# Modulation weights of the latent feed-forwards loaded through GpSimd's queue, their sums ordered behind the newest low part

## The chip, the core and the metric

One core of a Trainium2 chip runs the whole program. The metric is the time of one execution on the device in microseconds (us). Three timed runs of the kernel before are shown, and one more execution was profiled.

## The reference

Two layers run over 256 latent tokens of width 1024 (with 256 context tokens in the first layer only). Each layer is feed-forward, mixer, feed-forward, and each of these three is wrapped the same way:

```python
def sublayer(h, m, i, fn, res_w):
    y = fn(modulate(h, m[3 * i], m[3 * i + 1]))        # h * (1 + scale) + shift
    return layer_norm(ALPHA * h + res_w * m[3 * i + 2] * y, ln_g[l, i], ln_b[l, i])

def swiglu(h, w_in, w_out):                            # 1024 -> 2 x 2816 -> 1024
    gate, up = jnp.split(h @ w_in, 2, axis=-1)
    return (jax.nn.silu(gate) * up) @ w_out

m_lat = jnp.split(silu(c) @ w_ada[l] + b_ada[l], 9)    # nine vectors of 1024 a layer
```

The nine modulation vectors of a layer are products of one row, silu(c), with a 1024 x 9216 matrix. All numbers are float32.

## The kernel before

Every large matrix product is done in three passes: weights and activations are each split into a high part (rounded to the fast format) and a low part (the rest), and TensorE adds high x high, high x low and low x high (`mm3`, L209). A weight load brings 128 x 2048 floats (1 MB) into one of three buffers `raw` (L129, on SyncE's queue). ScalarE casts 1024 columns of it into `wh` (L150), VectorE subtracts and so makes the low part `wl` (L151). Here 1024 columns with their `wh` and `wl` are called a weight part; six buffers each hold them, and `wnext` makes parts five ahead of the one in use (`AHEAD`).

A latent feed-forward (`sub_ffn` and `ffn` with T = 2; there are three, in the order (0,1), (1,0), (1,1)) uses 66 weight parts: 44 for the first product, four to a pair of columns `ff`, and 22 for the second. TensorE makes `lf` (gate and up for 128 tokens), ScalarE applies SiLU and VectorE multiplies (`lsgf`, L469 and L470), TensorE transposes the product a little later (`ltrf`, `turn_last`, L435), and it is split again.

Beside this run the modulation vectors of later steps. `ada_jobs` lists them: for each vector eight units, and a unit is a load of 128 x 1024 floats (512 KB, `load`, L236, tile `ada`) and a sum on VectorE (`unit`, L240): the load times the row silu(c), summed over the 1024. After eight units `fin` (L248 on) adds the bias on GpSimd, and for a gate sends the vector to memory and back to spread it over the partitions (`gd`, `grow`). In the latent feed-forwards there are two buffers for the loads (`NADS`). `pace(44)` spreads the listed sums evenly over 44 steps. `bgstep` counts a step after each weight part from the third pair of columns on, that is from the 9th part, and calls `bg_one` when a sum is due; this issues the loads of the next two units and the sum.

At the start of a latent feed-forward `flush` (L377) puts out the scaling of `h` by the gain and bias of the layer norm before, `affine` (L368): on GpSimd, for each of two token tiles, a load of the gain row (512 KB, L372), two products, a load of the bias row into the same buffer, and two additions (L375). They stand behind `last_pow`, which there is GpSimd's share of the split of the normalized tokens (L217).

The order on each engine's queue is fixed when the program is put together: an instruction that is ready early can stand in front of one that is written earlier. `tc.issue_after(i)` puts what is written inside it behind instruction i, if it is on the same engine. `behind_x` does so for the split of the tokens.

Of the kernel before, what the change touches and what calls it, by code (L numbers as in the profile page):

```python
# [66 lines left out]
def body(ctx: ExitStack, tc: tile.TileContext, out, a):  # L67
    nc = tc.nc
    act, dve, pool, pe = nc.scalar, nc.vector, nc.gpsimd, nc.tensor
# [12 lines left out]
    def mmt(name):  # L82
        return mmp.tile([P, 512], F32, tag="mm", name=name)
# [16 lines left out]
    def col(name, i=0, n=1):  # L100
        return cols[:, CO[name] + i: CO[name] + i + n]
# [12 lines left out]
    ready = []  # L114
# [22 lines left out]
    lo_ins = {}  # L137
# [84 lines left out]
    bg = []  # L222
    cur_ada = [None]
    NADS = [3]

    def ada_jobs(l, v, streams, gate=None, then=None):


        for s in streams:
            mcol[l, v, s] = colp.tile([P, 8], F32, name=f"m{l}{v}{s}")  # L230
        for j in range(8):
            st = {}

            def load(j=j, st=st):
                st["raw"] = cur_ada[0].tile([P, D], F32, tag="adaraw", name=f"ada{l}{v}{j}", bufs=NADS[0])
                nc.sync.dma_start(st["raw"], a["wada"][l, v, j])  # L236

            def unit(j=j, st=st):
                for s in streams:
                    dve.scalar_tensor_tensor(st["raw"] if s == streams[-1] else crow["junk"], st["raw"], 1.0, crow[s], ALU.mult, ALU.mult,  # L240
                                             accum_out=mcol[l, v, s][:, j:j + 1])

            bg.append((load, unit, len(streams)))

        def fin():
            for s in streams:
                m = mcol[l, v, s]
                pool.tensor_tensor(m, m, col("bad", (l * 9 + v) * 8, 8), ALU.add)  # L248
                if gate is None:
                    continue  # L250
                if gate != 1.0:
                    pool.tensor_scalar(m, m, gate, None, ALU.mult)

                dr = drp.tile([P, 8], F32, name=f"gd{l}{v}{s}")
                pool.dma_start(dr, m)
                mrow[l, v, s] = (rowp if v == 5 else cur_ada[0]).tile([P, D], F32, tag=f"grow{s}", name=f"grow{l}{v}{s}", bufs=1)
                pool.dma_start(mrow[l, v, s], dr.rearrange("p j -> (p j)").partition_broadcast(P))
            if then is not None:
                then()

        bg.append((None, fin, 0))

    rate = [0.0, 0.0]

    def bg_one():
        for pre, _, _ in bg[:NADS[0]]:
            if pre is not None and id(pre) not in done:
                done[id(pre)] = pre
                pre()
        with behind_x():  # L270
            bg.pop(0)[1]()


# [2 lines left out]
    @contextmanager  # L276
    def behind_x():
        with ExitStack() as st:
            for i in anchors:
                st.enter_context(tc.issue_after(i.ins))  # L280
            yield
# [84 lines left out]
    last_pow = [None]  # L366
# [10 lines left out]
    def flush(after=None):  # L377
        with tc.issue_after((after or last_pow[0]).ins):
            while later:
                later.pop(0)()  # L380
# [19 lines left out]
    def ffn(st, l, i, T, parts, gv, prep, finish, lead):  # L400
# [43 lines left out]
        for p0, p1 in parts:  # L444
            for ff in range(p0, p1, 2):
                q = ff - p0
                if T == 4:
                    for j in range(2):
                        if ff + j in pre:
                            gps, ups = pre.pop(ff + j)  # L450
                        else:
                            gps, ups = mmt(f"g{nm}{ff}{j}"), mmt(f"u{nm}{ff}{j}")
                            group(gps)
                            group(ups)
                        act_mul(gps, ups, gslice(q + j, 1, slice(0, W)), 1, f"{nm}{ff}{j}")
                elif ff % 4 == 0 or ff > LEAD:

                    pairs = [ff, ff + 2] if ff < LEAD else [ff]
                    ps = {(f, t): mmt(f"l{nm}{f}{t}") for f in pairs for t in range(T)}
                    sg = {f: tp.tile([P, T, 256], F32, tag="t2", bufs=2, name=f"lsg{nm}{f}") for f in pairs}  # L460
                    ws = {}
                    seq = [(ff, t, j) for j in range(4) for t in range(T)]
                    if len(pairs) > 1:

                        seq = [(f, t, j) for t in range(T) for f in pairs for j in range(4) if f == ff or j < 2]
                        seq += [(ff + 2, t, j) for j in (2, 3) for t in range(T)]

                    def gate(f, t):
                        act.activation(sg[f][:, t, :], ps[f, t][:, 0:256], AF.Silu)  # L469
                        dve.tensor_tensor(sg[f][:, t, :], sg[f][:, t, :], ps[f, t][:, 256:512], ALU.mult)  # L470

                    for f, t, j in seq:
                        if (f, j) not in ws:
                            ws[f, j] = wnext((4, 3, 2, 1, 2, 1)[len(ws)] if ff == 0 and len(ws) < 6 else AHEAD)
                            if ff:
                                bgstep()
                        for k in (2 * j, 2 * j + 1):
                            with ExitStack() as after:
                                if ff == 0 and k % 2 == 0 and (f, t, j) != seq[0]:
                                    after.enter_context(tc.issue_after(last_mm[0].ins))  # L480
                                out_mm(ps[f, t], t, XH, XL, 0, k, k % 2, ws[f, j], k == 0, k == KT - 1)
                        if (f, t, j) == (0, 0, 3) and pend:
                            with behind_x(), tc.issue_after(nrm[0].ins):
                                pump_split(taken[0] + 2)
                            with tc.high_priority(HP), tc.issue_after(last_mm[0].ins):
                                to_x(*pend.pop())

                        if (f, t, j) == (2, 0, 1):
                            with behind_x():
                                gate(0, 0)  # L490
                        if j == 3 and (f, t) != (0, 0):
                            gate(f, t)
                            if t == T - 1:
                                turn_last()
                                turns.append((sg[f], q + f - ff, f))
                    if ff == 0:
                        flush()
            final = p1 == NFF
            for n in range(2):
                if final and n == 1:  # L500
                    while bg:
                        bg_one()
                    prep()
                pss = [mmt(f"o{nm}{p0}{n}{t}") for t in range(T)]
                qs = list(range(p0, p1, 2))
                hold = []
                for qi, k0 in enumerate(qs):
                    hold.append((k0, wnext(AHEAD + max(0, qi - 8) if T == 2 and final and n == 1 else AHEAD)))
                    bgstep()
                    if qi == 2:  # L510
                        turn_last()
                    if final and n == 1 and len(qs) - HOLD <= qi < len(qs) - 1:
                        continue
                    for t in range(T):
                        for kq, w in hold:
                            for kk in range(2):
                                gh, gl = gslice(kq + kk - p0, 1, slice(t * P, (t + 1) * P))
                                out_mm(pss[t], 0, gh, gl, 0, 0, kk, w, kq == p0 and kk == 0, kq == qs[-1] and kk == 1)
                        if qi == len(qs) - 1:
                            with tc.high_priority(HP if final else 0):  # L520
                                evac(pss[t], t, n, mrow[gv(t)], final and n == 1, ALPHA if p0 == 0 else 1.0,
                                     f"{nm}{p0}{n}{t}", f"{nm}{t}" if final else None)
                                if final and n == 1:
                                    finish(t)
                    hold = []
# [108 lines left out]
    with ExitStack() as st1:  # L634
# [38 lines left out]
        def prep():  # L673
            pass
# [242 lines left out]
    def sub_ffn(l, i, gates, mods, ln, nxt):  # L917
        with ExitStack() as st:
            cur_ada[0] = st.enter_context(tc.tile_pool(name=f"ada{l}{i}", bufs=1, side="right"))
            NADS[0] = 2  # L920
            for (gl, gv, f) in gates:
                ada_jobs(gl, gv, (0,), gate=f)
            for ml, mi, mln in mods:
# [368 lines left out]
```

## Time and profile before

| | us |
|---|---|
| timed runs | 1233.27, 1236.50, 1236.87 |
| median | 1236.5 |
| profiled execution | 1233.74 |
| its span, first instruction to last | 1231.9 |
| first latent feed-forward, about | 526 to 708 |
| second latent feed-forward, about | 715 to 906 |
| third latent feed-forward, about | 1037 to 1224 |

The profile is of one execution. An engine is busy while it runs an instruction; the time between two instructions is put down to what released the second one. PE is TensorE (PEld its weight loads), DVE VectorE, ACT ScalarE, POOL GpSimd, SP SyncE, which issues DMAs. PEclk is the granted share of TensorE's full clock of 2.4 GHz; 0.50 is 1.2 GHz. Times of a row count from the start of the span.

### The profile page before, as it was taken

The numbers are of one execution on the slowest core, as the hardware profiler recorded it, in microseconds if no ns is written. First come the engines' busy times: TensorE is split into PE (matmuls) and PEld (weight loads), VectorE is DVE, ScalarE is ACT, GpSimd is POOL, SyncE is SP. The second block draws the span as 40 slices with busy tenths as digits, with TensorE's granted clock in tenths as the row PEclk, the third lists the DMA queues.
The fourth block names the chain that finished last, engine by engine and source line by source line (L and its number), as shares of the span: only waits on it lengthen the run. The fifth ranks groups of instructions, "written<-read, shape, count | busy, mean of one in ns | idle before, by whom it ended". The sixth has DMA issues, their size and how long they took to land.

```text
span 1231.9 us, 14930 instructions
## 1 busy us (share of the span) xinstructions
PE 1181.1 (96%) x5632; PEld 979.7 (80%) x5632; DVE 882.7 (72%) x1287; ACT 503.2 (41%) x731; POOL 206.7 (17%) x207
## 2 busy tenths in 40 slices
PE   6999999999999999999999999997999888999997
PEld 5888888888887887778888878886879877888885
DVE  5799987773337858798785688877667957875554
ACT  4243123222233546564444444433448333544431
POOL 0001020031003122134010033000017911330000
PEclk9899999999999999999999999998999989999999
DMA  9778688862232432369885748987648445975550
GB/s 361 306 252 290 230 275 308 271 223 100 86 124 65 161 137 103 137 233 336 329 299 186 265 167 337 326 315 274 220 164 297 145 178 168 322 279 184 175 188 35
DMA packets 59656, 272.60 MB, mean 221 GB/s; under 512 B 6592, under 2 KB 8256, under 8 KB 44224
## 3 DMA queue, kind: packets, MB, share of 16 engines
q1 hardware_dynamic: 56048, 259.56, 59.2%
q0 software_dynamic: 3536, 12.09, 3.0%
q8 instruction: 44, 0.72, 0.2%
q14 instruction: 28, 0.23, 0.1%
HBM read 269.38 MB, written 1.08 MB: 220 GB/s over the span
## 4 chain that ended last, share of the span: by engine, by line
PE 48%; DVE 7%; DMA 6%; ACT 2%; issue 2%; POOL 1%; DVEq 0%; SPq 0%; ACTq 0%; POOLq 0%
PE lf L212 7%; PE lf L210 6%; PE lf L211 6%; DMA ada<-in_wada 6%; PE of L210 4%; PE of L212 4%; PE of L211 4%; PE pc L1137 2%; DVE wl L151 2%; DVE ada L240 1%; PE c L210 1%; PE c L211 1%; PE c L212 1%; PE ltrf L435 1%; PE v L210 1%
## 5 line engine op out<-in xcount | busy, mean ns | idle before, releaser
L150 ACT CAST wh<-raw 128x1024 fp32r<-128x1024 f32 x309 | 321.6, 1051 | 466.6 <-PE of L212 128.3
L151 DVE TENSOR_TENSOR wl<-raw,wh 128x1024 fp32r<-128x1024 f32 x302 | 379.2, 1271 | 150.3 <-ACT wh L150 149.3
L210 PE MATMUL lf<-wh,XH 128*128 128x512 f32 x528 | 208.5, 395 | 3.8 <-ACT XH L217 3.6
L240 DVE SCALAR_TENSOR_TENSOR ada<-ada,crow 128x1024 f32<-128x1024 f32 x128 | 163.1, 1282 | 68.3 <-DMA ada<-in_wada 67.6
L212 PE MATMUL lf<-wh,XL 128*128 128x512 f32 x528 | 207.0, 392 | 0.4 <-DVE XL L217 0.4
L211 PE MATMUL lf<-wl,XH 128*128 128x512 f32 x528 | 206.0, 390 | 0.0
L210 PE MATMUL of<-wh,GHf 128*128 128x512 f32 x344 | 135.1, 393 | 0.0
L212 PE MATMUL of<-wh,GLf 128*128 128x512 f32 x344 | 134.5, 391 | 0.0
L211 PE MATMUL of<-wl,GHf 128*128 128x512 f32 x344 | 134.5, 391 | 0.0
L210 PEld LDWEIGHTS lf<-wh,XH 128*128 128x128 f32 x528 | 99.2, 188 | 25.0 <-ACT XH L217 5.5
L212 PEld LDWEIGHTS lf<-wh,XL 128*128 128x128 f32 x528 | 99.1, 188 | 23.2 <-DVE XL L217 2.3
L211 PEld LDWEIGHTS lf<-wl,XH 128*128 128x128 f32 x528 | 99.2, 188 | 20.0
L211 PEld LDWEIGHTS of<-wl,GHf 128*128 128x128 f32 x344 | 65.0, 189 | 13.4
L212 PEld LDWEIGHTS of<-wh,GLf 128*128 128x128 f32 x344 | 64.9, 189 | 13.6
L210 PEld LDWEIGHTS of<-wh,GHf 128*128 128x128 f32 x344 | 65.0, 189 | 13.3
L248 POOL TENSOR_TENSOR m<-m,cols 128x8 f32<-128x8 f32 x19 | 13.9, 731 | 358.0 <-DVE ada L240 213.3
L210 PE MATMUL gf<-XH,wh 128*128 128x512 f32 x152 | 59.1, 389 | 0.0
L211 PE MATMUL gf<-XL,wh 128*128 128x512 f32 x152 | 59.1, 389 | 0.0
L212 PE MATMUL gf<-XH,wl 128*128 128x512 f32 x152 | 59.1, 389 | 0.0
L210 PE MATMUL uf<-XH,wh 128*128 128x512 f32 x152 | 59.1, 389 | 0.0
L211 PE MATMUL uf<-XL,wh 128*128 128x512 f32 x152 | 59.1, 389 | 0.0
L212 PE MATMUL uf<-XH,wl 128*128 128x512 f32 x152 | 59.1, 389 | 0.0
(296 smaller groups left out, 1948.2 us busy)
## 6 DMA issues: line engine op xcount, KB each, us to landing
raw<-in_wfl SPq DMA_DIRECT2D x66, 1024.0 KB, 6.8
ada<-in_wada SPq DMA_DIRECT2D x128, 512.0 KB, 5.4
raw<-in_wfo SPq DMA_DIRECT2D x40, 1024.0 KB, 5.0
raw<-in_wfi SPq DMA_DIRECT2D x22, 1024.0 KB, 6.2
raw<-in_wc SPq DMA_DIRECT2D x10, 1024.0 KB, 6.6
wcv<-in_wcv SPq DMA_DIRECT2D x16, 512.0 KB, 4.7
aw<-in_wsh SPq DMA_DIRECT2D x8, 512.0 KB, 10.4
aw<-in_wsc SPq DMA_DIRECT2D x8, 512.0 KB, 9.9
```

The costliest lines, as they stand in the source:

```text
L150: act.copy(wh[:, :w], r[:, off:off + w])
L151: lo_ins[q] = (pool if q in pool_lo else dve).tensor_tensor(wl[:, :w], r[:, off:off + w], wh[:, :w].bitcast(F32), ALU.subtract)
L210: pe.matmul(ps, lh, rh, start=first, stop=False)
L211: pe.matmul(ps, lh, rl, start=False, stop=False)
L212: last_mm[0] = pe.matmul(ps, ll, rh, start=False, stop=last)
L240: dve.scalar_tensor_tensor(st["raw"] if s == streams[-1] else crow["junk"], st["raw"], 1.0, crow[s], ALU.mult, ALU.mult, accum_out=mcol[l, ...
L248: pool.tensor_tensor(m, m, col("bad", (l * 9 + v) * 8, 8), ALU.add)
L435: pe.transpose(tr[:, j * W + t * P:j * W + (t + 1) * P], sg[:, t, j * P:(j + 1) * P], ident)
L1137: last = pe.matmul(pc[:, g * P:(g + 1) * P], wt[:, tap % 8 * P:(tap % 8 + 1) * P], z2, start=tap == 0, stop=tap == 15)
```

## The change

The modulation loads of the three latent feed-forwards are issued on GpSimd's queue instead of SyncE's; those of the first, four-tile feed-forward stay. The loop that issues the loads of the next units becomes a function, `bg_load`, of its own. It is called once more in the first pass over the columns (`ff == 0`), just before `flush`, so that the first two loads stand ahead of the scaling's loads on GpSimd's queue. And each sum of the latent feed-forwards is placed behind the newest low part that has been written up to there (`lo_ins[len(ready) - 1]`), so that it can't come in front of it on VectorE.

```diff
+    ada_queue = [nc.sync]
 ...
             def load(j=j, st=st):
                 st["raw"] = cur_ada[0].tile([P, D], F32, tag="adaraw", name=f"ada{l}{v}{j}", bufs=NADS[0])
-                nc.sync.dma_start(st["raw"], a["wada"][l, v, j])
+                ada_queue[0].dma_start(st["raw"], a["wada"][l, v, j])
 ...
-    def bg_one():
+    def bg_load():
         for pre, _, _ in bg[:NADS[0]]:
             if pre is not None and id(pre) not in done:
                 done[id(pre)] = pre
                 pre()
-        with behind_x():
+
+    def bg_one():
+        bg_load()
+        with behind_x(), ExitStack() as st:
+            if ada_queue[0] is pool:
+
+                st.enter_context(tc.issue_after(lo_ins[len(ready) - 1].ins))
             bg.pop(0)[1]()
 ...
                     if ff == 0:
+                        with tc.issue_after(last_pow[0].ins):
+                            bg_load()
                         flush()
 ...
             NADS[0] = 2
+            ada_queue[0] = pool
```

## Rows read from the trace of the kernel before

**Rows 1.** The page: busy time, share of the span and count of instructions
```profile
PE 1181.1 (96%) x5632; PEld 979.7 (80%) x5632; DVE 882.7 (72%) x1287; ACT 503.2 (41%) x731; POOL 206.7 (17%) x207
```
**Rows 2.** Busy time by stretch; the second line names the columns
```profile
core 0: us, PE busy (x) PEld busy (x) DVE busy (x) ACT busy (x) POOL busy (x), PEclk, DMA share, GB/s
536.00:700.00 164.00, 164.00 (x743) 135.31 (x744) 126.07 (x151) 79.59 (x100) 24.83 (x23) 1.00 0.79 283
724.00:846.00 122.00, 121.36 (x554) 99.99 (x554) 98.43 (x128) 54.98 (x75) 21.44 (x21) 1.00 0.87 316
846.00:855.00 9.00, 2.40 (x10) 1.42 (x9) 7.96 (x12) 4.53 (x7) 0.43 (x2) 0.80 0.83 300
855.00:858.00 3.00, 3.00 (x9) 2.41 (x9) 3.00 (x4) 0.59 (x1) 2.44 (x4) 0.50 0.55 158
```
**Rows 3.** Waits, 724 to 906: total, times, longest; sums: busy, mean ns, idle
```profile
PE ltrf L435 <- DVE lsgf L470: 7.2, 3, 5.4
...
L240 DVE SCALAR_TENSOR_TENSOR ada<-ada,crow 128x1024 f32<-128x1024 f32 x32 | 42.7, 1335 | 24.4 <-DMA ada<-in_wada 24.4
```
**Rows 4.** VectorE in order of time: start, us, [idle before, releaser]
```profile
846.73 1.23 DVE L240 SCALAR_TENSOR_TENSOR ada<-ada,crow 128x1024 f32<-128x1024 f32 x1 [3.54 <-DMA ada<-in_wada]
...
849.02 1.22 DVE L240 SCALAR_TENSOR_TENSOR ada<-ada,crow 128x1024 f32<-128x1024 f32 x1
...
850.16 2.36 DVE L151 TENSOR_TENSOR wl<-raw,wh 128x1024 fp32r<-128x1024 f32 x2
852.44 0.41 DVE L470 TENSOR_TENSOR lsgf<-lsgf,lf 128x256 f32<-128x256 f32 x1
853.16 1.23 DVE L240 SCALAR_TENSOR_TENSOR ada<-ada,crow 128x1024 f32<-128x1024 f32 x1 [0.31 <-DMA ada<-in_wada]
```
**Rows 5.** Waits of SyncE's queue, 724 to 860: total, times, longest
```profile
SPq L129 <- DVE wl L151: 46.1, 23, 6.1
...
SPq L236 <- DVE ada L240: 37.3, 15, 5.0
```
**Rows 6.** ScalarE's casts of weight parts, second and first latent feed-forward
```profile
744.33 1.06 ACT L150 CAST wh<-raw 128x1024 fp32r<-128x1024 f32 x1 [1.43 <-PE lf L212]
747.05 1.06 ACT L150 CAST wh<-raw 128x1024 fp32r<-128x1024 f32 x1 [1.66 <-PE lf L212]
...
555.98 1.06 ACT L150 CAST wh<-raw 128x1024 fp32r<-128x1024 f32 x1 [1.56 <-PE lf L212]
```
**Rows 7.** GpSimd in order of time, second and first latent feed-forward
```profile
727.09 0.65 POOL L372 DMA_DIRECT2D ln_g<-in_ln_g  x1
734.24 4.53 POOL L375 TENSOR_TENSOR h<-h,ln_g 128x512 f32<-128x512 f32 x2 [6.50 <-DMA ln_g<-in_ln_g]
...
750.17 0.57 POOL L372 DMA_DIRECT2D ln_g<-in_ln_g  x1 [0.30 <-POOL h L375]
754.87 2.57 POOL L375 TENSOR_TENSOR h<-h,ln_g 128x512 f32<-128x512 f32 x2 [4.12 <-DMA ln_g<-in_ln_g]
757.74 0.59 POOL L372 DMA_DIRECT2D ln_b<-in_ln_b  x1 [0.30 <-POOL h L375]
764.84 2.53 POOL L375 TENSOR_TENSOR h<-h,ln_b 128x512 f32<-128x512 f32 x2 [6.51 <-DMA ln_b<-in_ln_b]
...
571.18 0.59 POOL L372 DMA_DIRECT2D ln_b<-in_ln_b  x1 [0.30 <-POOL h L375]
576.22 2.53 POOL L375 TENSOR_TENSOR h<-h,ln_b 128x512 f32<-128x512 f32 x2 [4.45 <-DMA ln_b<-in_ln_b]
```
**Rows 8.** DMA, 715 to 860: `ada` loads, then others, KB, median us to landing
```profile
DMA to landing us min/median/max: 3.4/5.8/8.2
...
ln_g<-in_ln_g POOLq DMA_DIRECT2D x2, 512.0 KB, 5.8
ln_b<-in_ln_b POOLq DMA_DIRECT2D x2, 512.0 KB, 7.1
grow<-gd POOLq DMA_DIRECT2D x2, 512.0 KB, 7.0
```

## Prediction

> **What bounds the kernel now.** I read the page first, then the busy time by stretch. TensorE is busy for 96% of the span [rows 1], so a change on other engines can only win back the little time in which it stands still, or make more of it. The stretches say where that is: in the first latent feed-forward TensorE never stops (164.00 us of 164), in the second it loses 0.64 us of 122, then it is busy for 2.40 us of 9, and after that it runs for 3 us at a granted clock of 0.50, which is the lower of its two levels, 1.2 GHz [rows 2]. The list of waits names the cause: the transposes `ltrf` waited 7.2 us for the products `lsgf`, once for 5.4 us [rows 3]. VectorE's order around that place shows why the product was late. A sum of modulation weights starts at 846.73 after VectorE has stood still for 3.54 us until its weights landed; then come a low part, a sum at 849.02, two low parts, and only at 852.44 the product [rows 4]. VectorE works in order, so a sum whose weights are late holds up everything behind it. In this feed-forward its sums waited for their weights 24.4 us in all [rows 3].
>
> Why do they land late? SyncE's queue carries both streams. A weight load that waits for a free buffer (46.1 us in total) holds the modulation load behind it, and modulation loads that wait for a sum (37.3 us) hold the weight loads [rows 5].
>
> So what can be won is 7.2 us of standing still and the slow stretch behind it. 743 recorded matmuls in 164 us make 0.221 us each; nine of them took 3.00 us at the lower clock, where 9 x 0.221 = 2.0 us would do: 1.0 us. Together 8.2 us. No other wait of TensorE in the latent feed-forwards goes back to the sums.
>
> **The change, part by part.** *Loads moved off SyncE.* 64 loads (24, 32 and 8 in the three feed-forwards). SyncE no longer waits for sums. That gives earlier weights, but I credit nothing beyond the 8.2 us, since TensorE stands still nowhere else for it.
>
> *Loads put on GpSimd.* An issue there takes 0.57 to 0.65 us [rows 7]; 32 of them are some 20 us on an engine that is busy for 21.44 us of 122 [rows 2], so its time is not the question. Its order is. GpSimd too works in order, and at the start of each latent feed-forward it has the row scalings of the layer norm: four times a load of 512 KB, a wait for it, and two products. In the second feed-forward that chain runs from 727.09 to 764.84 + 2.53 = 767.4, in the first until 576.22 + 2.53 = 578.8 [rows 7]. The new `bg_load` puts the first two modulation loads ahead of it, which shifts it by two issues and by what two more transfers in that queue take; I count 2 us, with 1.3 (the issues alone) as the lower bound and 4 as the upper. The third load can't go ahead: there are two buffers, and it waits for the first sum.
>
> *Sums placed behind the newest low part.* Take the 66 weight parts of one latent feed-forward in the order of use. `bgstep` begins with the 9th, and step s has made 12 + s low parts. In the second feed-forward 32 sums over 44 steps are 0.727 a step, so sums 1 to 5 stand behind low parts 14, 15, 17, 18 and 19; in the first (24 sums, 0.545 a step) behind 14, 16, 18, 20 and 22. Until now sums ran ahead of their turn: three of the 32 are left at 846.7 [rows 4], so 29 are done there, where the new order has asked for 28 even at the stalled transposes. Those few sums less help at the old stall, and the same order costs at the start. With six buffers, part k is cast when TensorE is done with part k - 6. The 16th cast was released by TensorE at 744.33, the 17th at 747.05: 2.72 us a part, and part 10 done at 744.33 [rows 6]. The 14th low part then falls at about 741, so the first sum ends near 742.5, 15 us after GpSimd began its chain. The third load becomes ready when the chain is well under way.
>
> Where it stands in GpSimd's order the trace cannot show. Earliest: behind the third scaling load, 750.17 + 2 = 752.2. Latest: behind the whole chain, 769.4. In between lies the place behind the fourth scaling load, 757.74 + 2 + 0.6 = 760.3. I take that for the third load and the chain's end for the fifth, since its sum comes three steps later.
>
> How long does a load take to land? From SyncE 3.4 to 8.2 us, median 5.8; GpSimd's loads of the same size in this stretch had medians of 5.8, 7.1 and 7.0, mean 6.6 [rows 8]. I take 6.5 for these first loads, which meet the scaling loads, and 6.2, midway between 5.8 and 6.6, for the later ones.
>
> *Second feed-forward.* Sum 3 blocks the 18th low part. TensorE needs it when part 17 is done, 744.33 + 7 x 2.72 = 763.4, so the sum (1.23 us) and the low part (1.2) must start by 760.9 or so. The third load lands at 760.3 + 6.5 = 766.8: 6 us late. Load 5 issues behind the chain at 770.0, lands at 776.5, and its sum should have started by 766.4 (two parts later than 760.9): 10 us late. The latenesses don't add up, the largest counts: 10 us. Bounds: nothing if the third load goes at 752.2 and the following ones with it; 769.4 + 0.6 + 7.1 - 760.9 = 16 us if all stand behind the chain.
>
> *First feed-forward.* Part 10 done at 555.98 [rows 6]; part 18 at 577.7, so sum 3 should start by 575.2. The third load behind the fourth scaling load: 571.18 + 2.6 + 6.5 = 580.3, 5 us late. Bounds: 0 and, behind the chain, 578.8 + 2.6 + 7.1 - 575.2 = 13 us. I take 5.
>
> *Clock.* Each such stop costs the lower clock again, 1.0 us by the row above: 2.0.
>
> *The rest of the second feed-forward.* Its lead used up, TensorE goes as fast as the sums. Two buffers give two sums in 1.23 + 0.2 + 6.2 = 7.63 us; the pace asks for two in 2 x 2.72 / 0.727 = 7.48. That is 0.07 us a sum, 2 us over 27 sums. Bounds: 0 at 5.8 us a load, 13 us at 7.1. In the first feed-forward the pace is 2 x 2.72 / 0.545 = 10 us and the lead comes back. In the third, with 8 sums, the third load is asked for at about the 29th part, after the chain: nothing.
>
> *Sum.* -8.2 + 10 + 5 + 2.0 + 2 = +10.8 us. The profiled execution took 1233.74 us (span 1231.9 and 1.8 around it), so 1244.5. It lies 2.8 us below the median of the three runs, 1236.5, and within their spread (1233.27 to 1236.87); I leave the figure.
>
> **A rule that speaks against the change.** The rows first: GpSimd's scaling loads were issued in 0.57 to 0.65 us while VectorE was busy for 98 us of 122 [rows 2, 7]. The Trainium skill (SBUF — State Buffer, section "SBUF: two separate sides") says that GpSimd writes the descriptors of its DMAs itself and is shut out of a port shared with VectorE while VectorE runs certain fast modes; by that, loads from GpSimd would start late. In these rows no issue was held up, so the sum leaves it at nothing. As a mechanism of this kernel: if each issue had to wait out a VectorE instruction, 1.23 us, two sums would take 8.86 us, 0.69 us a sum above the pace, some 19 us over 27: 1263.
>
> **The rivals.** *Faster.* GpSimd's order lets the third and later loads in early, or the chain is shorter than now because fewer sums and loads run beside it. Then the first sums are in time, the old stall goes, and the time is 1233.7 - 8.2 = 1225.5. It decides at the third load: landed by 761 in the second feed-forward and by 575 in the first. For it: the scaling loads landed in 4.7 us at 754.87 [rows 7], and a load at 752.2 + 4.7 would be in time. Against: the chain runs to 767.4 now, and one queue is worked in order.
>
> *Traded.* The stall moves from the end of the second feed-forward to its start at about the old size, and the first one's lead covers it: -8.2 + 8 + 1 = +0.8, 1234.5. The Trainium skill (DMA: Bandwidth & Descriptors, section "Issuing engines are not separate DMA queues") holds that DMAs from any engine share the same 16 DMA engines and that another issuer saves only issue time; taken alone that is this rival, loads no faster and waits elsewhere. The similar landing times of rows 8 agree.
>
> *Much slower.* Loads at 7.1 us, as the scaling loads had, or the descriptor rule: 1244.5 + 11 = 1255.5 to 1263.
>
> **How the numbers follow.** Forecast 0.40, faster 0.28, traded 0.18, much slower 0.14 (0.03 of it the descriptor rule). What a measurement of this kernel can tell from no change is 0.3%, 3.7 us around 1236.5. Faster 0.28; same 0.18; slower 0.40 + 0.14 = 0.54. The forecast's own range, from its bounds, is 1240 to 1252. The range for 8 in 10 takes in the faster case and most of the much slower one: 1225 to 1258.
>
> **What would show it.** On GpSimd: where the third modulation load stands among the scaling products, and its issue time (forecast 760 in the second feed-forward, 574 in the first). On VectorE: a long wait for modulation weights before the third to fifth sum of each of the two. On TensorE: waits for low parts `wl` some 40 to 60 us into these feed-forwards instead of `ltrf` at 852; clock 0.50 behind them. I am wrong if the third load goes ahead of the third scaling product, or lands in under 5 us, or if TensorE stays busy throughout both.

## The result, and the profile after

The changed kernel takes 1252.27 us (median of four runs, 1247.81 to 1253.65) beside 1234.89 us for the kernel before on the same chip (four runs, 1233.27 to 1236.87): 1.0141 times as long, 95% interval 1.0122 to 1.0160, some 17.4 us. It is slower, as forecast, by 6.6 us more than the forecast's 10.8. The profiled execution took 1252.35 us, its span 1250.6 beside 1231.9.

The page, in the row that answers to [rows 1], then busy time by stretch of the changed kernel, and the kernel before in stretches cut alike. In each stretch the count behind PE busy is the number of matmuls.

```profile
PE 1187.1 (95%) x5632; PEld 983.9 (79%) x5632; DVE 874.9 (70%) x1287; ACT 502.8 (40%) x731; POOL 239.0 (19%) x271
```
```profile
536.00:700.00 164.00, 164.00 (x742) 135.33 (x743) 121.34 (x150) 78.65 (x99) 35.05 (x47) 1.00 0.81 289
...
724.00:775.00 51.00, 47.48 (x203) 38.69 (x202) 32.09 (x36) 24.08 (x32) 19.90 (x20) 0.93 0.69 255
775.00:860.00 85.00, 79.08 (x359) 64.23 (x357) 63.79 (x89) 33.52 (x47) 15.83 (x28) 1.00 0.81 298
860.00:866.00 6.00, 4.18 (x15) 2.96 (x14) 4.43 (x8) 2.48 (x3) 0.53 (x1) 0.76 0.98 354
866.00:904.00 38.00, 38.00 (x168) 31.43 (x167) 27.53 (x34) 13.16 (x13) 5.73 (x9) 0.99 0.60 219
```
```profile
724.00:775.00 51.00, 51.00 (x233) 42.03 (x233) 45.32 (x54) 27.01 (x37) 19.93 (x17) 1.00 0.83 308
775.00:860.00 85.00, 77.76 (x347) 63.42 (x346) 66.07 (x92) 33.50 (x46) 4.39 (x9) 0.96 0.87 310
860.00:866.00 6.00, 6.00 (x29) 4.94 (x28) 2.95 (x3) 2.65 (x3) 0.00 (x0) 1.00 0.62 195
866.00:904.00 38.00, 38.00 (x169) 31.49 (x168) 25.02 (x24) 17.51 (x18) 0.00 (x0) 1.00 0.72 260
```

Both kernels run the same 5632 matmuls in the same order, so the k-th of the one can be set beside the k-th of the other; the counts of the rows say roughly the same, to a matmul or two (some 0.22 us each) at every cut. The first latent feed-forward loses nothing (164.00 busy in both): at 724 the changed kernel is 0.1 us behind. At 775 it is 6.6 us behind, so 6.5 are lost there. From 775 to 866 it loses only 1.1 us more, to 7.8, but there the kernel before has its old stall. What the two lose in that stretch is read against a run told below (three buffers and the rows spread out), in which TensorE never stops there: the old stall cost 9.7 us (forecast 8.2), the changed kernel loses 10.8. At 904 it is still 7.8 us behind, at the last eviction of the whole kernel 14.7: 6.9 us have come in after 904. The chain that ended last, row for the last eviction, before and after:

```profile
1223.70 0.70 DVE evf L386
```
```profile
1238.38 0.70 DVE evf L393
```

And 4.0 us more lie behind it: span less that time is 8.2 us before and 12.2 after. In all 0.1 + 6.5 + 10.8 - 9.7 + 6.9 + 4.0 = 18.6 us, the difference of the spans. Each of these places has its row.

**To 775: the scaling chain.** GpSimd in order of time, the changed kernel, and VectorE beside it (each sum's read of its accumulator, 0.08 us, is left out here and below):

```profile
726.93 1.18 POOL L237 DMA_DIRECT2D ada<-in_wada  x2
728.10 0.53 POOL L379 DMA_DIRECT2D ln_g<-in_ln_g  x1
734.38 3.37 POOL L382 TENSOR_TENSOR h<-h,ln_g 128x512 f32<-128x512 f32 x2 [5.75 <-DMA ln_g<-in_ln_g]
...
753.41 2.54 POOL L382 TENSOR_TENSOR h<-h,ln_g 128x512 f32<-128x512 f32 x2 [4.14 <-DMA ln_g<-in_ln_g]
756.25 0.59 POOL L379 DMA_DIRECT2D ln_b<-in_ln_b  x1 [0.30 <-POOL h L382]
756.84 1.05 POOL L237 DMA_DIRECT2D ada<-in_wada  x2
761.00 2.48 POOL L382 TENSOR_TENSOR h<-h,ln_b 128x512 f32<-128x512 f32 x2 [3.11 <-DMA ln_b<-in_ln_b]
```
```profile
750.55 0.41 DVE L477 TENSOR_TENSOR lsgf<-lsgf,lf 128x256 f32<-128x256 f32 x1
762.30 2.26 DVE L241 SCALAR_TENSOR_TENSOR ada<-ada,crow 128x1024 f32<-128x1024 f32 x1 [11.34 <-DMA ada<-in_wada]
764.49 0.41 DVE L477 TENSOR_TENSOR lsgf<-lsgf,lf 128x256 f32<-128x256 f32 x1
```

The third and fourth modulation loads go out right behind the fourth scaling load, the place that the prediction took, 3.5 us earlier than it reckoned (756.84 for 760.3): the scaling rows landed sooner than in the kernel before, the last one's product began 4.75 us behind its issue where that took 7.10 [rows 7]. VectorE stands 11.34 us at sum 3, and the product that TensorE's transposes need stands behind it. TensorE stands for 3.5 us until 764.95, and then runs at the lower clock; the last stretch is at full clock again:

```profile
765.00:768.00 3.00, 3.00 (x8) 2.42 (x9) 3.00 (x5) 0.59 (x1) 0.43 (x1) 0.50 0.80 281
768.00:771.00 3.00, 3.00 (x9) 2.34 (x8) 2.38 (x4) 0.00 (x0) 0.53 (x1) 0.51 0.99 393
771.00:774.00 3.00, 3.00 (x15) 2.45 (x14) 2.46 (x4) 1.34 (x2) 0.53 (x1) 1.00 0.82 295
```

Of the 6.5 us, 3.0 are the slow clock's. The chain also holds up SyncE: a row for the convolution stage, `bcr`, shares the scaling rows' one buffer and stands in front of the weight loads until the chain frees it at 763.50; no weight load leaves from 749.85 to 766.06. In the kernel before, `bcr` goes at 848.62 and no wait for it is listed. It is not what stalls TensorE here: in the run with GpSimd's rows spread out it stands in the weights' way until 772.62, and this stall is gone.

**775 to 866: the gate's row.** The same view where the first gate is sent to DRAM and read back to all partitions:

```profile
783.93 0.60 POOL L256 DMA_DIRECT2D gd<-m  x1 [0.29 <-POOL m L253]
789.41 0.54 POOL L258 DMA_DIRECT2D grow<-gd  x1 [4.87 <-DMA gd<-m]
789.94 1.16 POOL L237 DMA_DIRECT2D ada<-in_wada  x2
```

GpSimd stands 4.87 us at a row load that waits for its own store, and two modulation loads leave as a pair behind it. The buffer of the earlier one was free from 786.5 on, when sum 9 ended, so that load is 3.4 us late; the later one's came free only at 790.3. In the first feed-forward GpSimd stands 8.11 us at the same place (608.66), in the second again 6.42 (826.15, one load 5.8 us late). TensorE's waits, in total, times and longest; the first answers to the first of [rows 3], the third is the kernel before's of the second:

```profile
PE ltrf L442 <- DVE lsgf L477: 11.3, 6, 3.5
PE tr L336 <- DVE h L322: 6.3, 3, 4.9
```
```profile
PE tr L329 <- DVE h L315: 2.3, 3, 1.1
```

**Behind 904: the last sums.** The last sum waits at 885.74 for its weights, with the low parts of the last weights behind it in VectorE's order; a raw buffer comes free only then, and ScalarE gets the next raw weights at 893.22:

```profile
885.74 1.23 DVE L241 SCALAR_TENSOR_TENSOR ada<-ada,crow 128x1024 f32<-128x1024 f32 x1 [4.26 <-DMA ada<-in_wada]
...
894.30 1.23 DVE L151 TENSOR_TENSOR wl<-raw,wh 128x1024 fp32r<-128x1024 f32 x1 [3.91 <-ACT wh L150]
```
```profile
893.22 2.95 ACT L150 CAST wh<-raw 128x1024 fp32r<-128x1024 f32 x3 [8.47 <-DMA raw<-in_wfo]
```

In the kernel before the last sum began at 853.16 [rows 4]. From 894 on the next stage's low parts run late too (909.81 to 918) and stand in front of the eviction; the second row of the waits above, 4.9 us of `tr` at 922, is where TensorE pays, and its granted clock is 0.81 on average from 912 to 930 (0.99 from 866 to 904).

**The end.** Instructions of the line that ends the program, on GpSimd, before and after; min, median and max in ns:

```profile
L1288 POOLq DRAIN  x3: 40/93/3564, 1226.3 to 1231.7; - x3
```
```profile
L1298 POOLq DRAIN  x3: 40/93/8791, 1241.0 to 1250.3; - x3
```

GpSimd's last drain takes 8.79 us in place of 3.56. It begins behind GpSimd's last operation, before the last output has landed, and before the change it ended inside that time; now the program waits for it alone. 5.23 us for 64 loads are 0.082 us each.

### The profile page after: what moved, and what is told of

It is laid out like the page before. It is cut to its first block, busy times and chain, and to the rows that moved or that the text cites. A ratio compares the mean times of both kernels' runs of the same rounds, so it can differ in the third digit from the quotient of the medians.

```text
span 1250.6 us, 14934 instructions
## 1 busy us (share of the span) xinstructions
PE 1187.1 (95%) x5632; PEld 983.9 (79%) x5632; DVE 874.9 (70%) x1287; ACT 502.8 (40%) x731; POOL 239.0 (19%) x271
## 3 DMA queue, kind: packets, MB, share of 16 engines
q0 software_dynamic: 12752, 45.65, 10.8%
## 4 chain that ended last, share of the span: by engine, by line
PE 42%; issue 7%; DMA 6%; DVE 6%; POOL 3%; ACT 2%; DVEq 0%; POOLq 0%; ACTq 0%
PE lf L212 6%; PE lf L210 6%; PE lf L211 6%; DMA ada<-in_wada 5%; PE of L212 3%; PE of L211 3%; PE of L210 3%; PE pc L1147 2%; DVE wl L151 1%; DVE ada L241 1%; DMA ln_g<-in_ln_g 1%; PE c L210 1%; PE c L211 1%; POOL h L382 1%; PE c L212 1%
## 5 line engine op out<-in xcount | busy, mean ns | idle before, releaser
L241 DVE SCALAR_TENSOR_TENSOR ada<-ada,crow 128x1024 f32<-128x1024 f32 x128 | 159.2, 1251 | 92.3 <-DMA ada<-in_wada 91.4
L237 POOL DMA_DIRECT2D ada<-in_wada x64 | 34.5, 540 | 193.2 <-DVE ada L241 193.1
```

The source lines that it names most:

```text
L237: ada_queue[0].dma_start(st["raw"], a["wada"][l, v, j])
```

## The experiments

The theory after this reading: the loads are late because GpSimd stands at its own rows (scaling, gate) with modulation loads queued behind, and a sum with late weights holds VectorE. Two rivals: the new place of the sums costs by itself; or loads from GpSimd's queue land late whatever stands in front of them. Ratios are to the kernel before on the same chip, 1232.9 to 1234.5 us.

**The order alone**
```
-            ada_queue[0] = pool
...
-            if ada_queue[0] is pool:
+            if NADS[0] == 2:
...
-                        with tc.issue_after(last_pow[0].ins):
-                            bg_load()
```


> Modulation loads back on SyncE, and no early loads; the sums stay behind the newest low part. Theory (GpSimd's order makes the loads late): 1235 to 1241 us, near the kernel before, with a TensorE stall at the end of the second latent feed-forward of some 7 us as before, and none near 765. Rival (the later place of the sums is what costs): 1246 us or more.

Measured: 1240.33 us, 1.0047 (1.0030 to 1.0064). Inside the theory's figure, but not by its picture: TensorE has stalls of 1.1 us at 769, 1.4 at 797 and 2.0 at 828, 2.8 of the old kind at 855, and `tr` waits 3.7 us at 913. Sum 5 waits 11.76 us before the first of them, and SyncE's queue shows why (its issues in order of time):

```profile
746.71 0.33 SPq L129 DMA_DIRECT2D raw<-in_wfl  x1
761.12 0.33 SPq L971 DMA_DIRECT2D bcr<-in_b_c  x1
761.50 0.42 SPq L237 DMA_DIRECT2D ada<-in_wada  x1
```

The row `bcr` stands in front of a modulation load here, until GpSimd's chain frees its buffer. The chain delays modulation loads on SyncE as well. So this run does not tell what the place of the sums costs by itself.

**The queue alone**
```
-            if ada_queue[0] is pool:
+            if False:
```


> Modulation loads on GpSimd's queue with the two early loads; the sums are not placed behind the newest low part. Theory (GpSimd's order): 1246 to 1254 us, near the changed kernel, with a long wait of VectorE for the third modulation load near 762. Rival (the later place of the sums): 1226 to 1236 us.

Measured: 1293.27 us, 1.0483 (1.0454 to 1.0511). Far beyond both. VectorE in order of time, this kernel:

```profile
772.29 1.23 DVE L241 SCALAR_TENSOR_TENSOR ada<-ada,crow 128x1024 f32<-128x1024 f32 x1 [7.94 <-DMA ada<-in_wada]
773.44 1.22 DVE L151 TENSOR_TENSOR wl<-raw,wh 128x1024 fp32r<-128x1024 f32 x1
775.62 1.27 DVE L241 SCALAR_TENSOR_TENSOR ada<-ada,crow 128x1024 f32<-128x1024 f32 x1 [0.96 <-DMA ada<-in_wada]
776.82 2.30 DVE L151 TENSOR_TENSOR wl<-raw,wh 128x1024 fp32r<-128x1024 f32 x1
781.92 1.23 DVE L241 SCALAR_TENSOR_TENSOR ada<-ada,crow 128x1024 f32<-128x1024 f32 x1 [2.80 <-DMA ada<-in_wada]
```

Left to itself the order has a sum between every two low parts. By the prediction's terms two buffers give a pair of sums in some 7.6 us, 3.8 us a sum, where a weight part takes 2.72: TensorE goes at the pace of the loads, in the first feed-forward too (150.30 us busy of 164). Given the queue, placing the sums gains some 41 us: with loads that are late, the second part of the change saves far more than it costs.

**No scaling rows in the second feed-forward**
```
-                    if ln != (1, 0):
+                    if ln not in ((1, 0), (0, 2)):
```


> The changed kernel without the four row loads and eight products of the layer norm at the start of the second latent feed-forward (that scaling is left out of the computation). Theory (the scaling chain stands in front of the third modulation load): the 3.5 us stall of TensorE at 765 and its slow clock are gone, 6.5 us less, 1244 to 1247 us; the third modulation load is issued before 746. Rival (loads from GpSimd's queue land late whatever stands in front of them): 1250 to 1254 us.

Measured: 1245.31 us, 1.0088 (1.0059 to 1.0117): 0.0053 x 1234.5 = 6.5 us less than the changed kernel's ratio, as the theory has it. The third load goes 1.5 us behind sum 1 (at 747.38, 743 without the late start told below). GpSimd now goes from the second load to the third with nothing between, and stands only for sum 1:

```profile
731.16 1.18 POOL L237 DMA_DIRECT2D ada<-in_wada  x2
747.38 0.53 POOL L237 DMA_DIRECT2D ada<-in_wada  x1 [15.05 <-DVE ada L241]
```

TensorE has no wait from 724 to 800 (the profiled execution, 1252.81 us, is the slowest of the eight; it runs 4.3 us late as a whole: it has a stall of 3.0 us in its first feed-forward, at 587, where the fourth and fifth load landed in 5.9 and 8.8 us, in the changed kernel's profile in 3.8 and 4.9). From 724 to 866 it falls 0.1 us further behind the kernel before, where the changed kernel falls 7.6. The later waits, at 826 and 853, and the 6.1 us of `tr` at 922 stay, and one of 1.6 us for a low part at 901 is new. This run takes away what holds `bcr` too.

**No wait for the gate's store**
```
-                pool.dma_start(dr, m)
+                if NADS[0] != 2:
+                    pool.dma_start(dr, m)
...
+                pool.dma_start(mrow[l, v, s], (a["ln_g"][0, 0] if NADS[0] == 2 else dr.rearrange("p j -> (p j)")).partition_broadcast(P))
```


> The changed kernel with the gate rows of the three latent feed-forwards loaded from a row of the layer norm's weights, without the store that the row load waits for (the computed gate rows are left out). Theory (GpSimd stands at the gate row's load while modulation loads are queued behind it): the TensorE stalls near 803 to 862 shrink, 3 to 6 us less, 1246 to 1249 us; the stall at 765 stays. Rival (only the scaling chain matters, the rest is the pace of two buffers): 1251 to 1254 us.

Measured: 1249.02 us, 1.0120 (1.0089 to 1.0152), some 3 us less than the changed kernel, at the edge of the theory's range; its interval and that of the changed kernel overlap. From 775 to 866 TensorE runs 396 matmuls, where the changed kernel runs 372 in one stretch cut alike, 24 more (5.3 us); 3.8 us of stall near 768 stay. A part of the gain goes again at the end, where `tr` waits 6.1 us.

**GpSimd's rows spread out** (nothing left out)
```
-        for pre, _, _ in bg[:NADS[0]]:
+        for pre, _, _ in [b for b in bg if b[0] is not None][:NADS[0]]:
...
+                            bg.insert(AT[p // 2], (None, both, 0))
...
+                    bg.insert(3, (None, rowload, 0))
```


> The changed kernel with GpSimd's order rewritten, nothing left out: each scaling row is loaded two sums before its products, the gate's row three sums after its store, and modulation loads are issued in front of them. Theory (GpSimd standing at its own rows makes the loads late): both kinds of stall go, 6.5 us at 765 and some 3 us behind the gate rows, 1240 to 1245 us, and less if the end of the second latent feed-forward recovers too. Rival (two buffers and loads of 4 to 9 us set the pace, whatever stands in front): 1248 to 1253 us.

Measured: 1241.48 us, 1.0058 (1.0036 to 1.0080). The stall at 765 is gone, with those near 803 and 862; two of 2.3 and 2.5 us are left at 830 and 852. Sums still wait up to 5.5 us for loads that landed in 8 to 9 us, the last one at 874, and `tr` waits 5.8 us at 912. From 724 to 866 it gains 1.1 us on the kernel before, where the changed kernel loses 7.6. So the rows in front were half of the 17.3 us lost up to there (8.7), and what is left comes with two buffers and such landings.

**Three buffers, the chain as it is**
```
-            NADS[0] = 2
+            NADS[0] = 3
...
-            row = rowp.tile([P, D], F32, tag="lnrow", name=f"{key}{l}{i}{t}")
+            row = xmp[0].tile([P, KT, P], F32, tag="xm", bufs=xmp[1], ...)
...
-        bcr = rowp.tile([P, D], F32, tag="lnrow", name="bcr")
+        bcr = cp.tile([P, D], F32, name="bcr")
```


> The changed kernel with three buffers for modulation weights in the latent feed-forwards (the scaling rows use the buffer of the transposed activations, which is free by then); GpSimd's chain stays. Theory (the third load waits for a buffer and then for the chain): the third load goes in front of the chain near 728, the fourth where the third was; the stall at 765 shrinks from 3.5 to under 1.5 us and later waits get a third buffer's slack, 1238 to 1245 us. Rival (the loads land late from this queue, or the order of the sums alone costs): 1248 us or more.

Measured: 1235.73 us, 1.0019 (1.0004 to 1.0035). The third load goes at 727.85. Sum 4 then waits 8.3 us for a load that stands where the third stood (756.87), and TensorE loses 1.2 and 1.6 us in two waits; the sums are done at 865.5, and `tr` at the end waits no longer than before, 1.1 us.

**Three buffers and the rows spread out** (both edits)

> Both: three buffers, and GpSimd's scaling and gate rows loaded well before their use. Theory (late loads are the whole loss): VectorE waits for no modulation load over 2 us, TensorE keeps busy through the second latent feed-forward, and the stall of the kernel before is gone as well: 1225 to 1233 us. Rival (the place of the sums costs by itself, as the order alone did with 5.9 us): 1236 to 1243 us.

Measured: 1229.89 us, 0.9970 (0.9959 to 0.9982): faster than before. Busy time by stretch, where [rows 2] have 121.36 and 2.40:

```profile
724.00:846.00 122.00, 122.00 (x559) 100.72 (x558) 103.04 (x133) 59.08 (x78) 37.63 (x51) 1.00 0.89 335
846.00:855.00 9.00, 9.00 (x44) 7.48 (x43) 6.91 (x9) 3.92 (x5) 1.06 (x2) 1.00 0.85 311
```

TensorE never stops there, with the sums behind the newest low part and the loads on GpSimd: neither the place of the sums nor the queue costs TensorE anything once the weights are in time. One sum still waits 4.3 us, without harm. Loads landed here in 7.1 us at the median, not sooner than before. That the rivals' mechanisms cost TensorE by themselves is out. The faster time is not all that TensorE gains: GpSimd's last drain takes 8.79 us here too, and span less the last eviction's time is 12.2 us.

**The last six sums left out**
```
+            if NADS[0] == 2 and v == 7:
+                pool.memset(mcol[l, v, s], 0.0)
...
+            if (l, i) == (1, 0):
+                del bg[29:35]
```


> The changed kernel without the last six modulation loads and sums of the second latent feed-forward (the six columns of the modulation vector that they would give are left at zero); the pace of the others is as before. Theory (the late sums near 866 to 887 hold the low parts of the last weights, and so TensorE's 4.9 us wait at 922): that wait falls under 1.5 us, 1244 to 1248 us. Rival (the wait at 922 comes from the low parts of the next stage or from the weight loads themselves): 1250 to 1254 us.

Measured: 1244.19 us, 1.0091 (1.0065 to 1.0118), in the theory's range. TensorE's waits from 900 to 935:

```profile
PE tr L338 <- DVE h L324: 1.7, 2, 1.1
```

The stalls at 766 and 804 are all there, and the wait at 922 is gone. So the wait at the end is the last sums' doing.

**The second feed-forward as before, the change in the first and third**
```
+                        if ada_queue[0] is pool:
...
-            ada_queue[0] = pool
+            ada_queue[0] = nc.sync if (l, i) == (1, 0) else pool
```


> The change in the first and third latent feed-forward alone; the second keeps its loads on SyncE and its sums unplaced, as in the kernel before. Theory (the loss on TensorE lies in the second alone, and the program's last drain of GpSimd grows by 0.082 us for each load that its queue carried, 32 of the 64 here): the stall of the kernel before comes back near 852, nothing else is lost before the end, and the end comes 2.3 us behind the last output's landing in place of 1.0 and 4.9: 1234.5 to 1237.5 us. Rival (loads from GpSimd cost in every feed-forward): 1240 us or more.

Measured: 1236.73 us, 1.0020 (1.0001 to 1.0039). In the profiled execution TensorE's old stall is back (4.9 us at 850) and nothing else; there the loss on TensorE is the second feed-forward's alone. That execution is the fastest of the ten (1231.78 us, the slowest 1242.95); where the others lose no trace shows. What is left over is 2.2 us in the medians; the end comes 2.3 us behind the last output's landing (1.0 before), as expected, so 1.3 of it is the drain. Its row here, with 32 of the 64 loads, and in the run without the last six sums, with 58:

```profile
L1299 POOLq DRAIN  x3: 40/102/6179, 1223.0 to 1229.7; - x3
```
```profile
L1302 POOLq DRAIN  x3: 40/93/8299, 1233.3 to 1242.1; - x3
```

0, 32, 58 and 64 loads give 3.56, 6.18, 8.30 and 8.79 us: 0.082 us a load throughout. The run without the four scaling rows, with 64, has 8.46: those rows count alike.

**Three buffers in the kernel before**, loads on SyncE, sums unplaced (the buffer edits as above)

> The kernel before with three buffers for modulation weights in the latent feed-forwards, nothing else: loads on SyncE, sums unplaced. Theory (two streams in SyncE's queue hold each other up, and a third buffer takes most of the modulation loads' waits away): the old stall of 7 us shrinks or goes, 1224 to 1231 us, and then GpSimd's queue is not what the best version gains by. Rival (the weight loads in the same queue hold the modulation loads up all the same): 1232 to 1236 us.

Measured: 1226.80 us, 0.9940 (0.9922 to 0.9958). By the medians the third buffer alone gains as much as the best versions. SyncE's queue, in total, times and longest, where [rows 5] have 46.1 and 37.3:

```profile
SPq L129 <- DVE wl L151: 87.2, 23, 7.3
SPq L236 <- DVE ada L240: 19.9, 8, 4.6
```

Its wait for sums is halved, the longer wait for weight buffers is slack (loads stand ready earlier), and of the 7.2 us of `ltrf` 1.8 are left. The edit moves `bcr` to a buffer of its own too; the two were not tried apart. The profiled execution is the slowest of the seven (1231.42 us): against the kernel before its TensorE gains 5.8 us from 724 to 904, where the versions with three buffers and spread rows on GpSimd's queue gain 9.5 and 9.7, and it loses 4.3 again behind that. Whether that queue gives TensorE more than the third buffer does, the medians do not show.

**Three buffers, rows spread out, sums unplaced**
```
-            if ada_queue[0] is pool:
+            if False:
```


> Three buffers and GpSimd's rows spread out, on GpSimd's queue, but the sums not placed behind the newest low part: then a sum stands behind nearly every low part. Theory (two buffers gave two sums in some 7.6 us, three give three in some 8.4, 2.8 us each against 2.7 us a weight part): most of the 59 us that the queue alone cost are gone, 1232 to 1250 us. Rival (a sum behind every low part is what costs, at any speed of the loads): 1265 us or more.

Measured: 1253.23 us, 1.0142 (1.0117 to 1.0166). The third buffer takes back 40 of the 59 us, less than the theory had. TensorE still waits 10.9 us for `lsgf` and 5.0 for low parts: with a sum behind nearly every low part TensorE has little lead, and landings of up to 9.4 us reach it; that this is the whole cause was not tried.

**Three buffers, GpSimd's queue in the second feed-forward only**
```
+                        if ada_queue[0] is not pool:
+                            flush()
...
-            ada_queue[0] = pool
+            ada_queue[0] = pool if (l, i) == (1, 0) else nc.sync
```


> Three buffers everywhere; in the second latent feed-forward GpSimd's queue, the sums' order and the spread rows; in the first and third loads on SyncE and sums unplaced. Theory (the second one alone gains, and each load on GpSimd costs 0.082 us at the last drain): 32 loads fewer give 2.6 us back, 1225.5 to 1228.5 us. Rival (the first and third gain from the queue too): 1230 us or more.

Measured: 1228.46 us, 0.9945 (0.9927 to 0.9963), 0.0025 or 3 us under the version with all 64 loads there, beside 2.6 from the drain. It cannot be told from the kernel before with three buffers, which is the simpler edit.

## Why the prediction was right, and where it was not

The forecast was slower by 10.8 us, for the reason that was found: GpSimd works in order, the third modulation load stands behind the scaling loads, VectorE waits for it, and TensorE behind VectorE. The measured 1252.27 us lies at the upper end of the forecast's own range (1240 to 1252). Step by step:

- **The old stall, -8.2.** Right: 9.7 us, gone in the changed kernel.
- **Second feed-forward's start, +10, and its clock, +1.** 6.5 us, but split otherwise: 3.5 of standing and 3.0 of slow clock. The third load stood where it was put, at 756.84 for 760.3, and landed in 5.4 us for 6.5. It alone made the stall. The fifth, which was to decide, went at 764.87 for 770.0; what released it was sum 3, whose buffer it takes, not the chain, whose products ended at 763.5 beside 767.4 [rows 7], since its rows landed sooner. Its sum waits 0.62 us. And the clock's 1.0 us was taken from 3 us of slow running [rows 2]; here TensorE ran for 6 us at 0.50.
- **First feed-forward's start, +5, and its clock, +1.** Nothing. The mechanism was right (sum 3 waits 9.05 us), but the load went at 567.43, not 574, and landed at 573.70 in place of 580.3. The sum began at 573.80, 1.4 us ahead of its latest start of 575.2. That margin is thin: the run without scaling rows in the second feed-forward, unchanged in the first, has a stall there.
- **The rest of the second feed-forward, +2.** The term that was mis-sized most: 10.8 us with its share of the clock. The pace of two buffers was reckoned with loads that leave as soon as a sum is done. The gate's store and row load are in GpSimd's order too; GpSimd stands at them for 4.87 and 6.42 us, and two loads leave 3.4 and 5.8 us after their buffers are free. The prediction used that row for its landing time [rows 8] and did not ask what waits behind it. That is the step that failed: of what stands in GpSimd's order only the scaling chain was counted. The gate's part of the 10.8 is some 5 us by one execution without the store; in the times it is not clear of noise.
- **After the feed-forward, nothing.** 6.9 us. Placing the sums behind low parts fixes the last one behind part 56 of 66; late, it holds the low parts of the last weights, and through the raw buffers the next stage's. In the kernel before the last sum stood 32.6 us earlier (853.16 for 885.74).
- **The end, nothing.** 4.0 us, the drain. It was not in any row that the prediction used.

Beside the forecast's terms that is 1.5 us more from the old stall, 4.5 and 6.0 less at the two starts, 8.8 more for the rest of the second feed-forward, and 6.9 and 4.0 that it did not have; with 0.1 before 724 this makes the 7.8 us from the forecast's 10.8 to the 18.6 of the profile. That the total is near is in part chance. Two of its figures do not come out of its own terms: at 7.1 us a load the bound for the rest is 14 us, not 13, and the bounds of its terms reach from -8 to some +36 us, far beyond the 1240 to 1252 that it calls the range from them.

The rivals: "traded" was about right for the old stall and the two starts alone, -9.7 + 6.5. The Trainium skill (DMA: Bandwidth & Descriptors, section "Issuing engines are not separate DMA queues") says that initiating DMAs on several engines saves only the time of initiating them; this case agrees for the transfers, whose median landing in the second feed-forward was 5.4 us from GpSimd and 5.8 from SyncE [rows 8]. The descriptor rule of the Trainium skill (SBUF — State Buffer, section "SBUF: two separate sides"), as a price on every issue, is not seen in the changed kernel: issues took 0.53 to 0.65 us while VectorE was busy for 96 of 136 us (724 to 860). TensorE's waits were named wrongly: they were `ltrf` for `lsgf`, not low parts `wl`, since in VectorE's order that product stood directly behind sum 3. TensorE missed it from 761.4 on, 2 us before the low part that the prediction timed.

## What to carry to other kernels

A queue that moves to another engine joins that engine's order: list every wait of that engine, stores that it reads back too, not the one chain that is nearest. When a consumer's loads are late by a round trip, first try one more buffer: here a third buffer (with `bcr` in one of its own) gave 0.994, the move with all its repairs, a third buffer among them, 0.997, with 4.0 us of drain in it. And an order that is pinned to other work carries lateness along to the end of the stage; ask where the last pinned piece falls.

## What the runs showed of the hardware

GpSimd's drain at the end of the program grows with the DMAs that it issued, by 0.082 us a load of 512 KB (3.56 us without them, 8.79 with 64), and once it outlasts the last output it is added to the time. GpSimd and VectorE also slow each other where they meet: sum 3 took 2.26 us beside GpSimd's products at 761.00, where sums take 1.23, and a pair of those products took 2.48 to 4.17 us. The four sums of the changed kernel's latent feed-forwards that took over 1.5 us all ran beside such products.
